# One fp32 transformer mixer layer on one core: another plan for sums of tokens, loads, the scale of q and the combining of output tiles

## The chip, the core and the metric

The kernel runs on one core of one Trainium2 chip. The metric is the time of one execution on the device in microseconds (us). The five engines are named as the profile names them: PE (TensorE, matrix products; PEld is its loading of weights), DVE (VectorE), ACT (ScalarE), POOL (GpSimd) and SP (SyncE, which here issues transfers only).

## What is computed

One layer over 512 tokens of 2048 channels, in fp32. Cut to what matters:

```python
h    = rms_norm(x, norm_g)
proj = h @ w_in                      # 512 x 2048 by 2048 x 8192
qa, ka, va, ga, qb, kb, vb, gb = split(proj)      # 8 + 8 heads of 128
ya = stick_breaking_attention(qa, ka, va)         # causal, no softmax
yb = chunk_band_attention(rms_norm(qb) , rms_norm(kb), vb, rel_bias)
mixed = concat(ya * silu(ga), yb * silu(gb))
out  = x + mixed @ w_out             # 512 x 2048 by 2048 x 2048
```

For the stick-breaking heads the weight of key s for query t is exp(log_sigmoid(z_ts) + the sum of log_sigmoid(-z_tj) over s < j < t). The chunked heads take a softmax over a band of nine chunks of 64 keys, with q and k normalised per head, gained, and a learned bias added.

## The kernel before

**Products.** Each fp32 operand is split into a high and a low part of type fp32r (`xh`, `xl` of the tokens, `wh`, `wl` of the weights), and a product is three matmuls, xh by wh, xl by wh and xh by wl (function `three`, lines 510 to 512). The two projections are made by a Winograd form of the 2x2 block product: seven products in the place of eight, of sums and differences of quarter blocks. The sums of weights (`wt`, lines 348, 351 and 352) and of tokens (`xt`, line 458, later split into `xh` and `xl` in lines 463 and 464) are made on DVE. ACT makes the high parts (line 370 for weights, 500 and 503 for tokens, where 503 multiplies by the norm's gain on the way), DVE the low parts (lines 374, 501 and 504).

**Units and steps.** The input projection has 32 units `u` of 256 output columns, four to a pair of heads (q, k, v, gate), the output projection four units of 512 columns (u = 32 to 35). A unit of the input projection has four steps (pairs j = 2r, 2r + 1 of the eight pairs of token tiles), one of the output projection eight. Units 0 and 1 are made in plain form and in turn, step by step, so that they need no sums of tokens (unit 32 is plain as well); unit 2 is the first that does. Weights of a step are loaded into one of three tiles `wt`, tokens of pair j into one of four staging tiles (`cq`, `ck`, `cv`, `cg`, which later hold the units' results). The four sums of pair j go into one tile, tag `v`, and the next pair's sums wait until they have been split.

**Results.** The products of a unit lie in halves of PSUM banks. Units 0, 1 and 32 are copied out by ACT (`copied`, line 625); all others are combined (`combine`): one ACT copy `U` (line 661), then six or seven DVE operations (lines 668, 676, 678, 679) that add and subtract the halves and free each for the unit that needs its bank next. The output projection has two row parts, a = 0 and 1, with tiles `wth` and `wtl` for results; x is added by transfers with accumulation that POOL issues (line 730), and SP stores the sum (line 735). For the last unit DVE and POOL add x.

**Attention.** While later units are multiplied, the heads of finished units are worked on: scores, for a stick-breaking head the chain ACT, POOL (a causal select, line 916), DVE scan (927), DVE subtraction (930), POOL select again, ACT exponential (933), then transposes on PE (1031), copies, and the product with the values. Sums of squares of x (`x_stats`, line 801) are made early on ACT from tiles `xs` that SP loads.

**Order.** There is no run-time scheduling. When the program is built, a planner simulates five engines and the transfers with a cost for each operation, and writes out a fixed order for each engine. An operation that is ready is taken by its due time; `need(k, d)` is the time at which product k will begin by the plan, less d, and `soon(d)` is d us from now. Costs on DVE and ACT are linear in the width. A transfer is planned to take its bytes by 330 bytes per ns, one after the other, and 2.2 us more to land. PE's next product is issued when its operands are there and nothing else is ready. An engine runs its list in order, and a wait of one instruction holds all that stand behind it.

The lines that matter most for what follows:

```python
WARM = 9                                                     # matmuls on zeros ahead of the first product
dma_free[0] = max(dma_free[0], clock[0] + op.cost) + op.lag / 330e3
return busy[engine] if op.quick else dma_free[0] + 2.2
yield lambda: "sums" not in done                             # sums of tokens: one tile
t = tmp([P, 4 * H], "v", f"xt{j}")
yield AC(H, lambda: act.activation(s_, s_, AF.Copy, scale=g_), need(k, 3.5))   # B12 of pair j
soon = lambda d: clock[0] + d                                # due time in combine
tag = ("wth", "wtl")[a]                                      # result tiles of the output projection
yield Op("SP", 0.94, gains, 25.0)                            # loads qg_t and kg_t
yield DV(1, lambda: dve.tensor_scalar(out=qgs, in0=qg_t, ...), 40.0)
```

Of the kernel before, what the change touches and what calls it, by code (L numbers as in the profile page):

```python
# [15 lines left out]
P = 128  # L16
# [43 lines left out]
WARM = 9  # L60
# [3 lines left out]
def trunk_kernel(ctx: ExitStack, tc: tile.TileContext, xT, xn, wi, wqk, wo, ng, qg, kg, rel, out):  # L64
# [62 lines left out]
    busy = dict.fromkeys(ready, 0.0)  # L127
    dma_free = [0.0]
# [44 lines left out]
    def issue(engine, op):  # L173
        op.fn()
        busy[engine] = clock[0] + op.cost
        if op.lag:
            dma_free[0] = max(dma_free[0], clock[0] + op.cost) + op.lag / 330e3

            return busy[engine] if op.quick else dma_free[0] + 2.2
        return busy[engine] + (0.17 if engine == "PE" else 0.1)  # L180

    def schedule(next_product):

        while True:
# [10 lines left out]
            for e in ready:  # L195
                if busy[e] > clock[0] + 1e-9:
                    continue
                if ready[e]:
# [140 lines left out]
    def landed_half(n, k, i, kk):  # L339
        at_ = dma_free[0] + 2.2  # L340
# [65 lines left out]
    def activations(j, mixed):  # L406
# [42 lines left out]
        else:  # L449
            yield lambda: "sums" not in done  # L450
            done.add("sums")
            t = tmp([P, 4 * H], "v", f"xt{j}")
# [3 lines left out]
            for o, i, g_, b_, op in ((0, 0, g1, q(r, 3), ALU.subtract), (1, 2, g2, q(r, 3), ALU.subtract),  # L456
                                     (2, 2, g2, q(t, 0), ALU.subtract), (3, 1, g2, q(t, 2), ALU.add)):
                yield DV(256, lambda: dve.scalar_tensor_tensor(out=q(t, o), in0=q(r, i), scalar=g_, in1=b_, op0=ALU.mult, op1=op,  # L458
# [7 lines left out]
        done.discard("sums")  # L466
# [27 lines left out]
    def raw_split(j, mixed, r, k, gain, x0, x1, names, h, l):  # L494
# [135 lines left out]
    def finish(u, a, t):  # L630
# [8 lines left out]
        done.remove(("co", a))  # L639

    def combine(u, a):
# [3 lines left out]
        soon = lambda d: clock[0] + d  # L645
# [17 lines left out]
        yield AC(512, first, soon(1))  # L663
# [4 lines left out]
        yield DV(256, lambda: dve.tensor_tensor(out=c[0][:, 1], in0=v(one(4)), in1=w[0], op=ALU.add), soon(1))  # L668
# [6 lines left out]
        else:  # L675
            yield DV(256, lambda: dve.tensor_tensor(out=c[0][:, 0], in0=w[0], in1=w[1], op=ALU.add), soon(1))
# [531 lines left out]
```

## Time and profile before

| what | value |
|---|---|
| median of three runs | 949.5 us (948.71 to 950.14) |
| the profiled execution | 950.14 us |
| its span, first to last instruction | 948.4 us |
| PE busy | 932.5 us (98%), 7377 matmuls |
| DVE busy | 830.0 us (88%) |
| ACT busy | 575.9 us (61%) |
| POOL busy | 80.3 us (8%) |
| granted TensorE clock, mean over the span | 0.997 |
| moved by transfers | 112.41 MB, 119 GB/s |

A busy share is an average over the whole span. The span is shorter than the execution's time by what lies before the first and behind the last instruction. PE counts as busy while any matmul is in flight, so that a PE that is busy all the time may still run at half of its clock; the granted clock of a stretch tells that.

### The profile page before, as it was taken

The numbers are of one execution on the slowest core, as the hardware profiler recorded it, in microseconds if no ns is written. First come the engines' busy times: TensorE is split into PE (matmuls) and PEld (weight loads), VectorE is DVE, ScalarE is ACT, GpSimd is POOL, SyncE is SP. The second block draws the span as 40 slices with busy tenths as digits, with TensorE's granted clock in tenths as the row PEclk, the third lists the DMA queues.
The fourth block names the chain that finished last, engine by engine and source line by source line (L and its number), as shares of the span: only waits on it lengthen the run. The fifth ranks groups of instructions, "written<-read, shape, count | busy, mean of one in ns | idle before, by whom it ended". The sixth has DMA issues, their size and how long they took to land.

```text
span 948.4 us, 19235 instructions
## 1 busy us (share of the span) xinstructions
PE 932.5 (98%) x7377; PEld 909.4 (96%) x7377; DVE 830.0 (88%) x1528; ACT 575.9 (61%) x1087; POOL 80.3 (8%) x157
## 2 busy tenths in 40 slices
PE   9899989999999999999999999999999999999997
PEld 7689989999999999999999999999999999999997
DVE  7789999988999989889999898899989987877875
ACT  6775856765467658654675576447768665534332
POOL 0001230000023000000230000002300000101010
PEclk9999999999999999999999999999999999999999
DMA  7742333223322332233223332422323445556471
GB/s 266 239 161 76 97 119 101 79 86 116 105 85 79 125 110 81 87 113 111 89 85 120 98 101 68 131 93 91 100 90 101 134 134 195 144 198 165 140 184 45
DMA packets 63916, 112.41 MB, mean 119 GB/s; under 512 B 7248, under 2 KB 11856, under 8 KB 63824
## 3 DMA queue, kind: packets, MB, share of 16 engines
q1 hardware_dynamic: 61680, 107.51, 35.2%
q0 software_dynamic: 1728, 3.15, 2.0%
q8 instruction: 57, 0.93, 0.4%
q10 hardware_dynamic: 416, 0.52, 0.2%
q14 instruction: 35, 0.29, 0.1%
HBM read 102.77 MB, written 8.39 MB: 117 GB/s over the span
## 4 chain that ended last, share of the span: by engine, by line
PE 56%; issue 27%; DVE 10%; DMA 4%; ACT 2%; POOL 1%; POOLq 0%; SPq 0%; DVEq 0%; ACTq 0%
PE banks L510 18%; PE banks L511 18%; PE banks L512 18%; DVE wl L374 3%; PE banks L1031 1%; DMA xs<-in_xn 1%; PE banks L959 1%; DMA co<-in_xn 1%; POOL W L916 1%; DMA x<-in_xT 1%; DVE wt L348 1%; ACT xs L801 1%; DMA qg_t<-in_qg 1%; DVE U L678 1%; DVE xt L458 0%
## 5 line engine op out<-in xcount | busy, mean ns | idle before, releaser
L510 PE MATMUL banks<-xh,wh 128*128 128x256 f32 (+1 forms) x1744 | 509.5, 292 | 3.2 <-ACT xh L500 1.6
L512 PE MATMUL banks<-xh,wl 128*128 128x256 f32 (+1 forms) x1744 | 501.3, 287 | 1.2 <-DVE wl L374 1.2
L511 PE MATMUL banks<-xl,wh 128*128 128x256 f32 (+1 forms) x1744 | 501.0, 287 | 0.5 <-DVE xl L501 0.5
L370 ACT CAST wh<-wt 128x1024 fp32r<-128x1024 f32 (+3 forms) x308 | 285.7, 937 | 242.4 <-PE banks L511 141.0
L374 DVE TENSOR_TENSOR wl<-wt,wh 128x768 fp32r<-128x768 f32 (+3 forms) x308 | 333.0, 1084 | 62.8 <-ACT wh L370 61.4
L510 PEld LDWEIGHTS banks<-xh,wh 128*128 128x128 f32 x1744 | 334.4, 192 | 7.8 <-ACT xh L500 2.4
L511 PEld LDWEIGHTS banks<-xl,wh 128*128 128x128 f32 x1744 | 334.2, 192 | 4.6 <-DVE xl L501 1.1
L512 PEld LDWEIGHTS banks<-xh,wl 128*128 128x128 f32 x1744 | 333.8, 191 | 5.0 <-DVE wl L374 2.4
L510 PE MATMUL banks<-wh,xh 128*128 128x256 f32 x432 | 122.7, 284 | 0.6 <-DVE co L679 0.5
L511 PE MATMUL banks<-wl,xh 128*128 128x256 f32 x432 | 122.3, 283 | 0.0
L512 PE MATMUL banks<-wh,xl 128*128 128x256 f32 x432 | 122.2, 283 | 0.0
L348 DVE TENSOR_TENSOR wt<-wt 128x512 f32<-128x512 f32 x144 | 99.4, 690 | 13.0 <-DMA wt<-in_wo 12.9
L510 PEld LDWEIGHTS banks<-wh,xh 128*128 128x128 f32 x432 | 82.9, 192 | 1.3 <-DVE co L679 1.2
L512 PEld LDWEIGHTS banks<-wh,xl 128*128 128x128 f32 x432 | 82.9, 192 | 0.0
L511 PEld LDWEIGHTS banks<-wl,xh 128*128 128x128 f32 x432 | 82.9, 192 | 0.0
L351 DVE TENSOR_TENSOR wt<-wt 128x256 f32<-128x256 f32 x144 | 61.1, 424 | 2.3
L352 DVE TENSOR_TENSOR wt<-wt 128x256 f32<-128x256 f32 x144 | 61.0, 424 | 2.0
L916 POOL TENSOR_SCALAR_AFFINE_SELECT W<-W 128x128 f32<-128x128 f32 x64 | 40.2, 629 | 98.4 <-DVE W L930 90.2
L916 POOL TENSOR_SCALAR_AFFINE_SELECT L<-L 128x128 f32<-128x128 f32 x32 | 21.8, 681 | 293.5 <-ACT L L922 286.3
L661 ACT COPY U<-banks 128x512 f32<-128x512 f32 x36 | 21.1, 585 | 23.9 <-PE banks L512 23.9
L1039 ACT CAST wth<-banks 128x128 fp32r<-128x128 f32 (+1 forms) x64 | 26.9, 421 | 10.4 <-PE banks L1031 10.4
L1031 PE MATMUL banks<-ident,W 128*128 128x128 f32 x160 | 29.2, 280 | 3.2 <-ACT W L933 2.5
(161 smaller groups left out, 1008.6 us busy)
## 6 DMA issues: line engine op xcount, KB each, us to landing
wt<-in_wi SPq DMA_DIRECT2D x254, 256.0 KB, 2.9
wt<-in_wo SPq DMA_DIRECT2D x64, 256.0 KB, 3.5
xs<-in_xn SPq DMA_DIRECT2D x16, 256.0 KB, 4.3
mixd<-c SPq DMA_DIRECT2D x16, 256.0 KB, 2.1
out<-co SPq DMA_DIRECT2D x16, 256.0 KB, 5.3
x<-in_xT SPq DMA_DIRECT2D x14, 256.0 KB, 4.5
co<-in_xn POOLq DMA_DIRECT2D x12, 256.0 KB, 7.2
bias<-in_rel SPq DMA_DIRECT2D x8, 256.0 KB, 3.3
```

Source lines behind the costliest of these rows:

```text
L348: yield DV(512, lambda: dve.tensor_tensor(out=some(t, 8, -7, 2), in0=some(t, 5, -5, 2), in1=some(t, 1, 0, 2), op=ALU.add), need(k0, 4))
L351: yield DV(256, lambda: dve.tensor_tensor(out=some(t, 9, 2), in0=some(t, 8, 2), in1=some(t, 0, 2), op=ALU.add), need(k1, 4))
L352: yield DV(256, lambda: dve.tensor_tensor(out=some(t, 12, 1), in0=some(t, 9, 2), in1=some(t, 4, 2), op=ALU.add), need(k1, 3.5))
L370: act.copy(whl[n, part][0][:, c], t)
L374: yield DV(c.stop - c.start, lambda: dve.tensor_tensor(out=l[:, c], in0=t, in1=h[:, c].bitcast(F32), op=ALU.subtract), need(k, 0.5))
L510: pe.matmul(o, lh, rh, start=start, stop=False, **kw)
L511: pe.matmul(o, lh, rl, start=False, stop=False, **kw)
L512: pe.matmul(o, ll, rh, start=False, stop=stop, **kw)
L661: act.copy(x[0], pair(u, a, 0, 1))
L916: pool.affine_select(out=x, in_=x, compare_op=ALU.is_gt, fill=fill, base=0, pattern=[[-1, P]], channel_multiplier=1)
L1031: pe.transpose(t[:, j * P:(j + 1) * P], src[:, j * P:(j + 1) * P], ident)
L1039: yield AC(w, lambda: act.copy(th[:, blocks, :], tv))
```

## The change

Eight edits, all in the planner's rules and costs or in where a value is kept; nothing else of the computation changes.

1. Eight matmuls on zeros ahead of the first product instead of nine.
2. Transfers are planned with 290 bytes per ns and 2.4 us to land. DVE operations with a scalar and two tensors (`STT`) are planned with 0.055 us more each.
3. The sums of tokens of pair j go into one of three tiles, `v`, `wth` or `wtl`, by j modulo 3. The first transposes of attention, which use `wth` and `wtl`, wait in turn for all eight pairs.
4. The scale of q's gain (`qgs`) is made only once 60 products have been issued.
5. The multiplication of the B12 part of pair 0 by the norm's gain goes from ACT to DVE.
6. In `combine` an operation that frees a bank is due by the next use of that bank (`next_use`), if that comes sooner than before.
7. After an operation of `combine` of the output projection, DVE takes for 0.2 us nothing that is due later than 1.5 us from then (`hold`).
8. Results of the output projection have four tiles: `wth` and `wtl` for even units, `cv` and `cg` for odd ones.

```diff
-WARM = 9
+WARM = 8
...
+    RATE, LANDING = 290e3, 2.4
...
+    def STT(w, fn, due=None):
+        return Op("DVE", 0.13 + 1.04e-3 * w, fn, due)
...
-            dma_free[0] = max(dma_free[0], clock[0] + op.cost) + op.lag / 330e3
-
-            return busy[engine] if op.quick else dma_free[0] + 2.2
+            dma_free[0] = max(dma_free[0], clock[0] + op.cost) + op.lag / RATE
+
+            return busy[engine] if op.quick else dma_free[0] + LANDING
...
+                    if clock[0] < held[e] - 1e-9 and k[0].due() > clock[0] + 1.5:
+                        continue
...
+                    if op.hold:
+                        held[e] = busy[e] + 0.2
+                        later(held[e], lambda: None)
...
-            yield lambda: "sums" not in done
-            done.add("sums")
-            t = tmp([P, 4 * H], "v", f"xt{j}")
+            tag = ("v", "wth", "wtl")[j % 3]
+            yield lambda: ("sums", tag) not in done
+            done.add(("sums", tag))
+            shape = [P, 2, S] if tag == "v" else [P, 13, P]
+            t = tmp(shape, tag, f"xt{j}").rearrange("p a b -> p (a b)")[:, :4 * H]
...
-                    yield AC(H, lambda: act.activation(s_, s_, AF.Copy, scale=g_), need(k, 3.5))
+                    if j:
+                        yield AC(H, lambda: act.activation(s_, s_, AF.Copy, scale=g_), need(k, 3.5))
+                    else:
+                        yield DV(H, lambda: dve.tensor_scalar(out=s_, in0=s_, scalar1=g_, scalar2=None, op0=ALU.mult), need(k, 3.5))
...
+    next_use, in_bank = {}, {}
+    for k in reversed(range(len(program))):
+        n, x, a = program[k]
+        u = steps_[n][0]
+        b = place(u, a, x[2]) // 2
+        if in_bank.get(b, (None, 0))[0] not in (None, (u, a)):
+            next_use[u, a, b] = in_bank[b][1]
+        elif b in in_bank and (in_bank[b][2] is not None):
+            next_use[u, a, b] = in_bank[b][2]
+        in_bank[b] = (u, a), k, next_use.get((u, a, b))
...
-            tag = ("wth", "wtl")[a]
-            yield lambda: ("co", a) not in done
-            done.add(("co", a))
+            tag = (("wth", "wtl"), ("cv", "cg"))[u % 2][a]
+            yield lambda: ("co", tag) not in done and emptied("cg", NG - 1)
+            done.add(("co", tag))
...
-        soon = lambda d: clock[0] + d
+        def soon(d, half=None):
+
+            t = clock[0] + d
+            k = None if half is None else next_use.get((u, a, place(u, a, half) // 2))
+            if k is None:
+                return t
+            wanted = need(k, 1.0)
+            return lambda: min(t, wanted())
...
+        def urgent(op):
+            op.hold = u >= NU
+            return op
...
-        yield DV(256, lambda: sub_(c[0][:, 1], v(one(6)), w[1]), soon(0.5))
+        yield urgent(DV(256, lambda: sub_(c[0][:, 1], v(one(6)), w[1]), soon(0.5, 6)))
...
-        yield lambda: ("turn", n, b - 1) in done if b else n == 0 or ("values", n - 1) in done
+        yield lambda: ("turn", n, b - 1) in done if b else ("values", n - 1) in done if n else all(("staged", j, 0) in done for j in range(NJ))
...
         yield Op("SP", 0.94, gains, 25.0)
+        yield lambda: position[0] > 60
         yield DV(1, lambda: dve.tensor_scalar(out=qgs, in0=qg_t, scalar1=SCALE, scalar2=None, op0=ALU.mult), 40.0)
```

What the planner makes of it is seen in the order of the instructions. At three places it is shown here; between the two kernels the line numbers differ (458 is 473 in the changed kernel, 464 is 479, 504 is 523, 501 is 520, 374 is 387, 348, 351 and 352 are 361, 364 and 365, 930 is 973).

**Place 1: DVE, in the steps of units 0 and 1.** `xl2` is the low part of token pair 2, `xt3` the sums of pair 3, `wl0_6` the low part of step 6's weights. Before:

```order
L464 TENSOR_TENSOR xl2_123<-xt2_333,xh2_122 128x1024
L1145 TENSOR_SCALAR qgs_72<-qg_t_70 128x1
L458 SCALAR_TENSOR_TENSOR xt3_396<-x3_124,ng_t_69 128x256 x2
L458 SCALAR_TENSOR_TENSOR xt3_396<-x3_124,ng_t_69,xt3_396 128x256 x2
L504 SCALAR_TENSOR_TENSOR xl6_367<-x6_365,ng_t_69,xh6_366 128x256
L501 TENSOR_TENSOR xl6_367<-x6_365,xh6_366 128x256
L464 TENSOR_TENSOR xl3_126<-xt3_396,xh3_125 128x1024
L374 TENSOR_TENSOR wl0_6_430<-wt6_286,wh0_6_429 128x1024
```

In the changed kernel:

```order
L473 SCALAR_TENSOR_TENSOR xt3_297<-x3_123,ng_t_69,xt3_297 128x256
L520 TENSOR_TENSOR xl5_236<-x5_234,xh5_235 128x256
L473 SCALAR_TENSOR_TENSOR xt3_297<-x3_123,ng_t_69,xt3_297 128x256
L387 TENSOR_TENSOR wl0_4_327<-wt4_249,wh0_4_326 128x1024
L523 SCALAR_TENSOR_TENSOR xl4_201<-x4_199,ng_t_69,xh4_200 128x512
L523 SCALAR_TENSOR_TENSOR xl5_236<-x5_234,ng_t_69,xh5_235 128x512
L473 SCALAR_TENSOR_TENSOR xt4_303<-x4_199,ng_t_69 128x256 x2
L473 SCALAR_TENSOR_TENSOR xt4_303<-x4_199,ng_t_69,xt4_303 128x256 x2
L479 TENSOR_TENSOR xl2_122<-xt2_222,xh2_121 128x1024
L479 TENSOR_TENSOR xl3_125<-xt3_297,xh3_124 128x1024
L387 TENSOR_TENSOR wl0_5_394<-wt5_275,wh0_5_393 128x1024
```

The last sum of pair 3 now stands ahead of step 4's weights and 14 rows ahead of the weights of step 6 (before 4 rows ahead of these); `qgs` stands 67 rows further down, behind the weights of step 12. SP's list at the same place, in the order of issue (`x7` is the load of pair 7, `wt8` of step 8). Before:

```order
L435 DMA x6_365<-in_xT 128x2x256
L436 DMA x6_365<-in_xT 128x512
L1141 DMA qg_t_70<-in_qg 128x1
L1142 DMA kg_t_71<-in_kg 128x1
L307 DMA wt8_382<-in_wi 128x512 x2
L796 DMA xs_393<-in_xn 128x512
L796 DMA xs_398<-in_xn 128x512
L796 DMA xs_409<-in_xn 128x512
L435 DMA x7_421<-in_xT 128x2x256
L436 DMA x7_421<-in_xT 128x512
```

In the changed kernel:

```order
L320 DMA wt6_313<-in_wi 128x512 x2
L448 DMA x6_317<-in_xT 128x2x256
L449 DMA x6_317<-in_xT 128x512
L448 DMA x7_344<-in_xT 128x2x256
L449 DMA x7_344<-in_xT 128x512
L320 DMA wt7_356<-in_wi 128x512 x2
L839 DMA xs_366<-in_xn 128x512
L839 DMA xs_369<-in_xn 128x512
```

Pair 7 is now loaded ahead of step 7's weights and of all tiles `xs`; before, step 8's weights and six tiles `xs` stood ahead of it.

**Place 2: DVE, where unit 34 ends and unit 35 begins.** `co34_1` is the result of unit 34's second row part, `wl0_153` and `wl1_153` belong to the second step of unit 35. Before:

```order
L679 TENSOR_TENSOR co34_1_11242<-banks_79,U_11233 128x2x128
L374 TENSOR_TENSOR wl0_153_11259<-wt153_11099,wh0_153_11258 128x1024
L678 TENSOR_TENSOR co34_1_11242<-banks_79,U_11233 128x2x128
L374 TENSOR_TENSOR wl1_153_11248<-wt153_11099,wh1_153_11247 128x768
L679 TENSOR_TENSOR co34_1_11242<-banks_79,U_11233 128x2x128
```

In the changed kernel:

```order
L721 TENSOR_TENSOR U_11230<-banks_79,co34_1_11239 128x512
L722 TENSOR_TENSOR co34_1_11239<-banks_79,U_11230 128x2x128
L721 TENSOR_TENSOR co34_1_11239<-banks_79,U_11230 128x2x128
L722 TENSOR_TENSOR co34_1_11239<-banks_79,U_11230 128x2x128
L387 TENSOR_TENSOR wl0_153_11257<-wt153_11096,wh0_153_11256 128x1024
L361 TENSOR_TENSOR wt154_11152<-wt154_11152 128x2x2x128
L387 TENSOR_TENSOR wl1_153_11245<-wt153_11096,wh1_153_11244 128x768
```

The two splits of weights have gone behind the last two operations that free banks.

**Place 3: DVE, behind the subtraction of the first stick-breaking head's third block of queries** (`W`, 384 keys), which POOL's second select waits for. Before:

```order
L930 TENSOR_TENSOR W_1099<-banks_79,W_1099 128x384
L348 TENSOR_TENSOR wt18_1080<-wt18_1080 128x2x2x128
L374 TENSOR_TENSOR wl1_17_1176<-wt17_1020,wh1_17_1175 128x768
L1117 TENSOR_TENSOR c3_1137<-c3_1137,R_78 128x1024
L883 TENSOR_TENSOR qk1_1205<-c0_537,qk1_1205 128x512
```

In the changed kernel:

```order
L973 TENSOR_TENSOR W_1129<-banks_79,W_1129 128x384
L365 TENSOR_TENSOR wt18_1059<-wt18_1059 128x256
L387 TENSOR_TENSOR wl0_18_1203<-wt18_1059,wh0_18_1202 128x1024
L361 TENSOR_TENSOR wt19_1110<-wt19_1110 128x2x2x128
L361 TENSOR_TENSOR wt20_1198<-wt20_1198 128x2x2x128
L364 TENSOR_TENSOR wt19_1110<-wt19_1110 128x2x128
L364 TENSOR_TENSOR wt20_1198<-wt20_1198 128x2x128
L365 TENSOR_TENSOR wt19_1110<-wt19_1110 128x256
```

Other operations follow the subtraction, and the transposes of this block stand 48 rows later in PE's list (row 648 instead of 600 of some 7120).

## Rows read from the trace of the kernel before

**Rows 1.** Busy time by stretch: PE, PEld, DVE, ACT, POOL, then granted clock, DMA, GB/s
```profile
30.00:40.00 10.00, 9.93 (x45) 7.91 (x43) 5.84 (x10) 6.24 (x13) 0.00 (x0) 1.00 0.86 257
40.00:50.00 10.00, 7.16 (x21) 4.98 (x22) 9.49 (x18) 7.71 (x19) 0.00 (x0) 0.83 0.73 245
50.00:60.00 10.00, 8.51 (x47) 7.21 (x45) 8.15 (x13) 7.69 (x16) 0.00 (x0) 1.00 0.57 181
60.00:100.00 40.00, 39.48 (x321) 38.75 (x322) 38.53 (x72) 24.00 (x42) 5.25 (x8) 1.00 0.30 99
100.00:150.00 50.00, 47.48 (x384) 46.42 (x383) 48.22 (x81) 35.91 (x68) 13.13 (x22) 1.00 0.30 96
150.00:200.00 50.00, 49.99 (x404) 48.93 (x403) 44.91 (x111) 35.05 (x95) 0.84 (x5) 1.00 0.31 96
```

**Rows 2.** Waits of PE: for whom, us in total, times, longest us
```profile
PE banks L1031 <- ACT W L933: 2.5, 2, 2.2
PE banks L510 <- ACT xh L500: 1.6, 1, 1.6
PE banks L510 <- ACT c L625: 1.5, 1, 1.5
PE banks L512 <- DVE wl L374: 1.2, 3, 0.7
PE banks L511 <- DVE xl L501: 0.5, 1, 0.5
```

**Rows 3.** Timeline of PE near 43 us: start, duration, instruction, idle before and releaser
```profile
43.47 0.49 PE L510 MATMUL banks<-xh,wh 128*128 128x512 f32 x1 [1.61 <-ACT xh L500]
```

**Rows 4.** Timeline of DVE near 36 us
```profile
35.96 0.15 DVE L1145 TENSOR_SCALAR qgs<-qg_t 128x1 f32<-128x1 f32 x1 [3.74 <-DMA qg_t<-in_qg]
```

**Rows 5.** Timeline of SP near 38 us
```profile
37.85 0.38 SPq L435 DMA_DIRECT2D x<-in_xT  x1
```

**Rows 6.** Timeline of ACT near 42 us and near 59 us
```profile
42.23 0.49 ACT L488 ACTIVATE x<-x,ng_t 128x256 f32<-128x256 f32 x1
...
58.81 0.63 ACT L801 ACTIVATE xs<-xs 128x512 f32<-128x512 f32 x1 [1.58 <-DMA xs<-in_xn]
...
59.43 0.57 ACT L625 COPY c<-banks 128x512 f32<-128x512 f32 x1
```

**Rows 7.** DMA issues by line (the page's part 6): KB each, median us to landing
```profile
xs<-in_xn SPq DMA_DIRECT2D x16, 256.0 KB, 4.3
```

**Rows 8.** Timeline of PE near 906 us
```profile
905.93 0.28 PE L512 MATMUL banks<-wh,xl 128*128 128x256 f32 x1
906.44 0.39 PE L510 MATMUL banks<-wh,xh 128*128 128x256 f32 x1 [0.23 <-DVE co L679]
```

**Rows 9.** Timeline of DVE near 905 us
```profile
905.10 0.94 DVE L374 TENSOR_TENSOR wl<-wt,wh 128x768 fp32r<-128x768 f32 x1
905.97 0.41 DVE L679 TENSOR_TENSOR co<-banks,U 128x256 f32<-128x256 f32 x1
```

**Rows 10.** Timeline of PE near 1 us and near 12 us
```profile
1.52 4.21 PE L1131 MATMUL banks<-zz 128*128 128x512 f32 x9 [1.52 <-DVE zz L1129]
...
12.79 0.50 PE L512 MATMUL banks<-xh,wl 128*128 128x512 f32 x1 [0.19 <-DVE wl L374]
```

**Rows 11.** Timeline of POOL near 120 us and near 140 us
```profile
120.68 2.42 POOL L916 TENSOR_SCALAR_AFFINE_SELECT W<-W 128x128 f32<-128x128 f32 x1 [4.16 <-DVE W L930]
...
140.21 1.15 POOL L916 TENSOR_SCALAR_AFFINE_SELECT W<-W 128x128 f32<-128x128 f32 x1 [2.06 <-DVE W L930]
```

**Rows 12.** Timeline of DVE near 122 us
```profile
120.47 0.41 DVE L351 TENSOR_TENSOR wt<-wt 128x256 f32<-128x256 f32 x1
120.80 1.22 DVE L374 TENSOR_TENSOR wl<-wt,wh 128x1024 fp32r<-128x1024 f32 x1
...
122.27 0.68 DVE L348 TENSOR_TENSOR wt<-wt 128x512 f32<-128x512 f32 x1
123.63 0.42 DVE L927 TENSOR_TENSOR_SCAN W<-L,W 128x128 f32<-128x128 f32 x1 [0.68 <-POOL W L916]
```

More of the change, by code (lines that the diff above doesn't have):

```diff
@@ L127, in trunk_kernel @@
     busy = dict.fromkeys(ready, 0.0)
+    held = dict.fromkeys(ready, 0.0)
     dma_free = [0.0]
@@ L139, in __init__ @@
             self.due = due if callable(due) else (lambda d=clock[0] + LATE if due is None else due: d)
+            self.hold = False
     LATE = 5.0
+    RATE, LANDING = 290e3, 2.4
     def DV(w, fn, due=None, n=1):
@@ L457, in activations @@
                                      (2, 2, g2, q(t, 0), ALU.subtract), (3, 1, g2, q(t, 2), ALU.add)):
[L458 removed]
+                yield STT(256, lambda: dve.scalar_tensor_tensor(out=q(t, o), in0=q(r, i), scalar=g_, in1=b_, op0=ALU.mult, op1=op,
                                                               reverse1=op == ALU.subtract), need(kt, dt + 4))
@@ L465, in activations @@
         done.update(("x", j, x, mixed) for x in ("T1", "T2", "T3", "T4"))
-        done.discard("sums")
+        if not mixed:
+            done.remove(("sums", tag))
         names = ("B11", "B21") + (("B12",) if not mixed or plain(NU, j) else ())
@@ L503, in raw_split @@
             yield AC((x1 - x0) * H, lambda: act.activation(h, s_, AF.Copy, scale=gain), need(k, 2.6))
-            yield DV((x1 - x0) * H, lambda: dve.scalar_tensor_tensor(out=l, in0=s_, scalar=gain, in1=h.bitcast(F32), op0=ALU.mult,
+            yield STT((x1 - x0) * H, lambda: dve.scalar_tensor_tensor(out=l, in0=s_, scalar=gain, in1=h.bitcast(F32), op0=ALU.mult,
                                                                     op1=ALU.subtract), need(k, 0.5))
@@ L661, in first @@
             act.copy(x[0], pair(u, a, 0, 1))
-        yield AC(512, first, soon(1))
+        yield AC(512, first, soon(1, 0))
         w = [v(x[0][:, i, :]) for i in range(2)]
@@ L667, in combine @@
         c, t = yield from result(u, a)
-        yield DV(256, lambda: dve.tensor_tensor(out=c[0][:, 1], in0=v(one(4)), in1=w[0], op=ALU.add), soon(1))
+        yield urgent(DV(256, lambda: dve.tensor_tensor(out=c[0][:, 1], in0=v(one(4)), in1=w[0], op=ALU.add), soon(1, 4)))
         free(4)
@@ L675, in combine @@
         else:
-            yield DV(256, lambda: dve.tensor_tensor(out=c[0][:, 0], in0=w[0], in1=w[1], op=ALU.add), soon(1))
+            yield urgent(DV(256, lambda: dve.tensor_tensor(out=c[0][:, 0], in0=w[0], in1=w[1], op=ALU.add), soon(1)))
         yield there(2, 3)
@@ L679, in combine @@
         add_ = lambda o, i, j: dve.tensor_tensor(out=o, in0=i, in1=j, op=ALU.add)
-        yield DV(512, lambda: sub_(v(x[0]), v(pair(u, a, 2, 3)), c[0][:, 1][:, None].to_broadcast(list(v(x[0]).shape))), soon(1))
+        yield urgent(DV(512, lambda: sub_(v(x[0]), v(pair(u, a, 2, 3)), c[0][:, 1][:, None].to_broadcast(list(v(x[0]).shape))), soon(1, 2)))
         free(2)
-        yield DV(256, lambda: add_(c[1][:, 1], v(one(3)), w[0]), soon(1))
+        yield urgent(DV(256, lambda: add_(c[1][:, 1], v(one(3)), w[0]), soon(1, 3)))
         free(3)
@@ L685, in combine @@
             yield there(5)
-            yield DV(256, lambda: add_(c[1][:, 1], c[1][:, 1], v(one(5))), soon(1))
+            yield urgent(DV(256, lambda: add_(c[1][:, 1], c[1][:, 1], v(one(5))), soon(1)))
             free(5)
@@ L709, in combine @@
         yield there(7)
-        yield DV(256, lambda: add_(c[1][:, 0], v(one(7)), w[0]), soon(0.2))
+        yield urgent(DV(256, lambda: add_(c[1][:, 0], v(one(7)), w[0]), soon(0.2, 7)))
         free(7)
@@ L877, in prep_a @@
         if kind == 0:
-            yield DV(512, lambda: dve.scalar_tensor_tensor(out=f, in0=f, scalar=SCALE, in1=R, op0=ALU.mult, op1=ALU.mult))
+            yield STT(512, lambda: dve.scalar_tensor_tensor(out=f, in0=f, scalar=SCALE, in1=R, op0=ALU.mult, op1=ALU.mult))
         else:
@@ L989, in prep_b @@
         yield AC(512, lambda: act.activation(d[:, 2 * kind, :], b, AF.Copy, scale=gain))
-        yield DV(512, lambda: dve.scalar_tensor_tensor(out=d[:, 2 * kind + 1, :], in0=b, scalar=gain, in1=d[:, 2 * kind, :].bitcast(F32),
+        yield STT(512, lambda: dve.scalar_tensor_tensor(out=d[:, 2 * kind + 1, :], in0=b, scalar=gain, in1=d[:, 2 * kind, :].bitcast(F32),
                                                       op0=ALU.mult, op1=ALU.subtract))
```

8 lines of the change are left out of this document (4 added, 4 removed).

## The prediction

> **What bounds the kernel now.** I read the page first: PE is busy 98% of the span, so time can only be won where PE stands or runs slowly. The stretches come next [rows 1]. From 30 to 40 us PE issues 45 matmuls of 512 columns in 10 us, one each 0.222 us, and from 150 to 200 us 404, nearly all of 256 columns, one each 0.124 us. Two stretches fall out: 40 to 50 us, with 21 matmuls, 7.16 us busy and a mean granted clock of 0.83 of 2.4 GHz, which is part of the stretch at 1.2 GHz; and 50 to 60 us, with 1.49 us idle. From 100 to 150 us 2.5 us are idle. The waits of PE say for whom [rows 2]: a low part of weights (three times, 1.2 us in all), token pair 7 (1.6 and 0.5 us), a copy of unit 1's result (1.5 us), an exponential of attention (two, 2.5 us).
>
> The reader is to follow the stop at 43.47 us back. PE waits for the high part of pair 7 [rows 3]; ACT began on pair 7 at 42.23 us [rows 6], since SP issued that load only at 37.85 us [rows 5], into the staging tile that pair 3 had to leave. Pair 3 is left when DVE has made its sums, and DVE came to them at 36 us: it had stood 3.74 us for a transfer of 512 bytes, q's gain, of which it makes `qgs`, a value first used in a chunked head much later [rows 4]. While PE stood its clock fell, and the matmuls after the stop ran at half of it.
>
> **The change, part by part.**
>
> *A. The early stop (edits 2, 3, 4).* `qgs` goes down 67 rows; nothing early then waits on that transfer. Sums in three tiles let pair 3's sums go ahead of step 4's weights, and SP issues pair 7 ahead of step 7's weights. The queues it moves past: on SP, the weights of steps 7 and 8 and six tiles `xs` now come after it; weights have three tiles and are loaded two steps ahead of their use, which hides that. On DVE the sums move ahead of weights that are needed later. Price of the stop: 45 less 21 matmuls are missing, 24 x 0.222 = 5.3 us [rows 1]. Bounds: 0 if another input is late in its place, 5.3 if none. I take 5.3: all three causes are moved by more than a step (24 matmuls of 0.222, 5.3 us), and DVE gets its 3.74 us back.
>
> *B. The copy of unit 1 (edit 2).* ACT stood 1.58 us for a tile `xs` and made the copy only at 59.43 us, for which PE waited 1.5 us [rows 2, 6]. The transfer takes 4.3 us [rows 7] and was planned with some 3.0 (262144 bytes by 330 per ns, and 2.2); 290 and 2.4 give 3.3, nearer but still short. Of the 16 squares 13 stood ahead of that copy, the last of them directly; now nine do, with a cast of weights between. Bounds 0 and 1.6 (1.5, and the longer matmul behind a stop); I take 1.2, nearer the upper end, since four transfers less must land before it.
>
> *C. Ends of units 33 and 34 (edits 6, 7, 8).* PE issues a matmul at 905.93 us and the next at 906.44, 0.51 instead of 0.124 later, and waits for DVE's last addition at 905.97 [rows 8]. Ahead of that stood a split of weights of 0.94 us [rows 9], and a longer one further ahead; both now stand behind it. 0.39 us a boundary, and 0.11 because the first matmul after a stop is longer (0.39 against 0.28): two boundaries, 1.0 us. Bounds 0 and 1.0; I take 1.0, since the addition comes 0.94 us or more sooner for a wait of 0.39. The two splits, of the next step's weights, are late next. Three sums of a later step's weights have gone from ahead of the first split (0.68, 0.42 and 0.41 us by their like in [rows 12]), more than the two additions that came ahead of it. The second split is needed eight products of three matmuls into its step, 24 x 0.124 = 3 us; without that cover PE would wait up to 0.94 us. Four result tiles hide nothing, as no row shows a wait for a result tile; edit 8 is 0.
>
> *D. The start (edits 1, 5).* Nine matmuls on zeros take 4.21 us, 0.47 each [rows 10]. But PE waits at 12.79 us for a low part of step 1's weights, ahead of which DVE has 18 operations before and 20 after, with one moved from ACT [rows 10]. DVE begins sooner by the ACT operation that has gone (0.49 for its like in [rows 6]) and has about as much more to do. So 0; bounds -0.5 (slower) and +0.5.
>
> *E. Attention's first heads (follows from all).* PE stood 2.2 us for an exponential, because POOL's select took 2.42 us, and another took 1.15 us [rows 2, 11]. While the first was held, DVE ran four operations with both operands in SBUF, the first at 120.47 and the last at 122.27 us, and then stood 0.68 us itself for that select [rows 12]. The new order deals these anew: other operations follow each subtraction. Bounds: +2.5 if no select is held, -8.1 if all three long runs hold one (the rival below). I take +1.0: of the eight subtractions of the first two heads two cost something before, 2.2 and 0.3 us, and I put in one stop between them, 1.5.
>
> The Trainium skill (page "SBUF — State Buffer", section "SBUF: two separate sides") says that a DVE instruction with two SBUF inputs and a GpSimd instruction that reads SBUF lock each other out, and that the later one waits for the whole instruction of the other. The trace agrees that POOL is blocked, but its 2.42 us go past the end of one DVE instruction of 1.22 us and into a fourth. By the rule a hold would end after 1.22 us at most, an estimate of 0.6 on the mean; PE's wait would be some 0.4 us instead of 1.5, and the forecast 1.1 us lower.
>
> *F. New short waits.* The first 60 us are dealt anew. The nearest row are the three waits for weights, 1.2 us in all [rows 2]; bounds 0 and 3.6, three times as many. I take one more such set, -1.2.
>
> Sum: 5.3 + 1.2 + 1.0 + 0 + 1.0 - 1.2 = 7.3 us off the profiled execution, whose span is 948.4 and whose time is 950.14 us. The median of the three runs is 949.5, 0.6 lower; taken from it, **942.2 us**. The end is untouched: the last PE matmul to the last store keep their order.
>
> **Rivals.**
>
> *DVE takes it back.* PE gets 5.3 + 1.2 - 1.2 = 5.3 us sooner into a stage where DVE is nearly full: idle 1.5 us of 40 and 1.8 of 50 [rows 1]. If DVE has only these 3.3 us to give until 150 us, 2.0 come back as waits for weights, and E's 1.0 is lost: 949.5 - 7.3 + 3.0 = 945.2. For it: 96% busy. Against: DVE also has the 3.74 us it stood, 5.1 us idle from 150 to 200, and the planner put attention later against the products (48 rows of PE, 6 us, at place 3), and level with before by about 200 us.
>
> *Another late input takes the place of pair 7.* Then A is lost and the rest stays: 949.5 - 7.3 + 5.3 = 947.5. For it: transfers still land later than planned, by 1.0 us for `xs`, and the transfer engines are 0.86 busy from 30 to 40 us [rows 1]. Against: pairs 5, 6 and 7 are each issued a step or more ahead.
>
> *The change gains nothing.* The edits move a plan, not work. If the rest of the program waits on loads, an earlier PE meets later weights, and only C stays: 948.5. For it: transfers land later than the plan has it, 4.3 against 3.3 us for `xs` [rows 7]. Against: the transfer engines are 0.31 busy from 150 to 200 us [rows 1], and no row of PE's waits names a transfer.
>
> *Slower: held selects.* In the new order three subtractions of the first two stick-breaking heads are followed by at least four operations with both operands in SBUF (by the durations of [rows 12], with 0.94 for a split of 768 columns [rows 9], 3.7, at least 4.2 and 3.3 us). If POOL is held through each, PE waits each time for 0.2 us less, as it did (2.2 of 2.42): 10.6 us instead of 2.5, E is -8.1 instead of +1.0, and DVE's own stops of 0.68 us make its weights late by 2.0 more: 949.5 - 7.3 + 9.1 + 2.0 = 953.3. It decides from 9.2 us of such waits on beyond the 1.5 in E. Against: such a run stood behind the third subtraction before as well (place 3), and only two waits are on record [rows 2].
>
> **How the numbers follow.** Forecast 0.65, DVE takes it back 0.13, another late input 0.08, nothing gained 0.07, slower 0.07. 0.2% are 1.9 us, about what a measurement of this kernel can tell from no change. Faster by more, below 947.6: the first two and three quarters of the third, 0.84. Within: the rest of the third and the fourth, 0.09. Slower: 0.07. The low end has A, the upper bounds of B, C and E and no new waits: 949.5 - 5.3 - 1.6 - 1.0 - 2.5 = 939.1, and with D's bound 938.6. The high end takes in the third case, 947.5. What lies outside is the fourth and fifth case and some of the third. The forecast's own range is 938.6 to 945.
>
> **What would show it.** A: from 40 to 50 us no clock below 1.00, some 45 matmuls of 512 columns, no wait for pair 7, `qgs` without a wait. B: no wait of PE for the copy of unit 1. C: PE's pitch at the two ends of units stays 0.12 us, DVE's splits behind the additions. D: PE's first products up to 0.5 us sooner, the wait near 12.8 us still there. E: selects above 1 us, and waits of PE for an exponential between 80 and 150 us. Wrong it would be with a second clock drop in the first 70 us, waits for low parts of weights between 60 and 200 us of over 2 us in all, or several selects above 2 us with PE behind them.

## The result, and the profile after

The changed kernel takes 942.65 us (median of 4, 942.48 to 942.99) against 949.71 us before on the same chip (4 runs, 948.71 to 950.14): ratio 0.9928, 95% interval 0.991 to 0.9945. Forecast were 942.2 us in 938.6 to 947.5. The profiled execution takes 942.50 us, its span is 940.4 us.

The page's header and busy line of the changed kernel:

```profile
span 940.4 us, 19231 instructions
PE 929.5 (99%) x7376; PEld 908.0 (97%) x7376; DVE 830.7 (88%) x1529; ACT 574.1 (61%) x1085; POOL 79.4 (8%) x157
```

Busy shares hardly move. The stretches, with the columns of [rows 1], changed kernel:

```profile
30.00:40.00 10.00, 10.00 (x45) 8.26 (x45) 9.38 (x17) 6.53 (x16) 0.00 (x0) 1.00 0.67 195
40.00:50.00 10.00, 10.00 (x46) 8.27 (x45) 10.00 (x16) 9.90 (x20) 0.00 (x0) 1.00 0.66 219
50.00:60.00 10.00, 10.00 (x82) 9.88 (x81) 9.93 (x16) 8.73 (x15) 0.00 (x0) 1.00 0.74 239
60.00:100.00 40.00, 39.56 (x327) 39.11 (x326) 38.25 (x74) 24.48 (x46) 5.36 (x11) 1.00 0.34 116
100.00:150.00 50.00, 49.22 (x397) 48.05 (x396) 46.00 (x80) 33.99 (x67) 14.73 (x19) 1.00 0.29 97
150.00:200.00 50.00, 49.31 (x392) 47.75 (x392) 43.50 (x110) 34.96 (x96) 0.84 (x5) 1.00 0.27 86
```

From 40 to 50 us there are 46 matmuls and a clock of 1.00, where [rows 1] have 21 and 0.83. From 50 to 60 us PE is never idle. But from 150 to 200 us it issues 392 instead of 404. PE's waits, columns as in [rows 2], changed kernel:

```profile
PE banks L1074 <- ACT W L976: 1.8, 6, 0.4
PE banks L529 <- DVE wtl L1083: 0.5, 1, 0.5
PE banks L531 <- DVE wl L387: 0.2, 1, 0.2
```

The waits for pair 7 and for the copy of unit 1, both in [rows 2], are gone. Two waits for an exponential, one of them 2.2 us long, have become six of at most 0.4 us.

To add this up I use PE's **lost time**: for each matmul the time from its start to the next one's start, less the median of that for its shape in the same trace, summed by stretch. It counts idle time, the longer first matmuls behind a stop, and matmuls at half clock alike. Worked out from the trace of every kernel here (us; the heads of the columns are us from the span's start, the last column is the span):

```
kernel              0-20  20-50  50-66 66-150 150-300 300-800  800-   all    span
before              3.46   5.60   1.78   4.52   1.56   4.24   1.57  22.73   948.4
changed             3.79  -0.04  -0.01   2.52   3.73   4.61   0.29  14.88   940.4
only_tiles          3.75  -0.05  -0.01   2.81   1.79   4.27   1.38  13.95   939.7
only_q_later        3.40   1.85   1.99   4.90   1.54   4.26   1.38  19.32   945.0
only_combine        3.57   4.15   3.55   6.00   1.54   4.25   0.06  23.12   948.8
q_from_ng           3.60   2.28   3.60   5.96   1.56   4.29   1.38  22.67   948.4
xs_later            3.81   0.94   0.31   9.68   2.93   4.29   1.35  23.31   949.0
q_ng_xs_later       3.63  -0.04   0.04   8.93   2.89   4.28   1.35  21.08   946.8
tiles_combine       3.58  -0.04  -0.01   5.01   1.74   4.14   0.06  14.48   940.2
undo_tiles          3.20   2.51  -0.01   1.96   1.70   4.37   0.59  14.32   939.8
undo_combine        3.90  -0.04  -0.01   3.20   3.74   4.52   2.79  18.09   943.6
undo_plan           3.59  -0.04  -0.01   3.46   1.75   4.35   0.06  13.16   938.6
undo_plan_select    3.61  -0.04   0.55   1.96   1.01   3.81   0.05  10.95   936.4
```

Lost time falls by 7.85 us, the span by 8.0: the table accounts for the gain. Each row is one execution, and not always a middling one: that of `only_q_later` took 946.73 us with a granted clock of 0.999, its median is 950.07.

### The profile page after: what moved, and what is told of

Its sections match the earlier page's. It is cut to its first block, busy times and chain, and to the rows that moved or that the text cites. A ratio compares the mean times of both kernels' runs of the same rounds, so it can differ in the third digit from the quotient of the medians.

```text
span 940.4 us, 19231 instructions
## 1 busy us (share of the span) xinstructions
PE 929.5 (99%) x7376; PEld 908.0 (97%) x7376; DVE 830.7 (88%) x1529; ACT 574.1 (61%) x1085; POOL 79.4 (8%) x157
## 4 chain that ended last, share of the span: by engine, by line
PE 61%; issue 24%; DVE 10%; ACT 2%; POOL 2%; DMA 0%; ACTq 0%; DVEq 0%; POOLq 0%
PE banks L529 19%; PE banks L530 19%; PE banks L531 19%; DVE wl L387 3%; POOL W L959 1%; PE banks L1074 1%; PE banks L1002 1%; DVE wt L361 1%; DVE W L970 1%; ACT wh L383 1%; DVE wtl L1083 1%; DVE wt L364 1%; PE banks L1110 0%; DVE W L973 0%; DVE wt L365 0%
## 5 line engine op out<-in xcount | busy, mean ns | idle before, releaser
L387 DVE TENSOR_TENSOR wl<-wt,wh 128x1024 fp32r<-128x1024 f32 (+3 forms) x308 | 333.9, 1085 | 69.7 <-ACT wh L383 65.7
L1083 DVE TENSOR_TENSOR wtl<-banks,wth 128x128 fp32r<-128x128 f32 (+1 forms) x64 | 30.8, 482 | 2.0 <-ACT wth L1082 2.0
```

The source lines that it names most:

```text
L387: yield DV(c.stop - c.start, lambda: dve.tensor_tensor(out=l[:, c], in0=t, in1=h[:, c].bitcast(F32), op=ALU.subtract), need(k, 0.5))
L1083: yield DV(w, lambda: dve.tensor_tensor(out=tl[:, blocks, :], in0=tv, in1=th[:, blocks, :].bitcast(F32), op=ALU.subtract))
```

## The experiments

The experiments were timed in three sets, on chips 12, 2 and 1, each with the kernel before beside it: 951.29, 951.26 and 950.89 us (medians of 26, 8 and 19 runs). Ratios are to that, with 95% intervals. The first set has `only_tiles`, `only_q_later`, `only_combine` and `q_from_ng`, the second `tiles_combine`, `undo_tiles`, `undo_combine` and `undo_plan`, the third the other four.

### Which edit takes the early stop away

**One edit alone, on the kernel before.** `only_tiles` is edit 3:

```diff
-            yield lambda: "sums" not in done
+            tag = ("v", "wth", "wtl")[j % 3]
+            yield lambda: ("sums", tag) not in done
```

> The kernel before with edit 3 alone, sums in three tiles. DVE still stands for q's gain. Theory: the sums of pair 3 are made before that stand, so pair 7 is loaded in time, but the low parts behind the stand are late: 1 to 3 us gained. Rival (the tiles are the cause): 4 to 5 us gained and no clock drop.

Measured: 942.04 us (941.37 to 944.16), ratio 0.9917 [0.9888, 0.9946]. `only_q_later` is edit 4:

```diff
+        yield lambda: position[0] > 60
         yield DV(1, lambda: dve.tensor_scalar(out=qgs, in0=qg_t, ...), 40.0)
```

> The kernel before with edit 4 alone, the scale of q made only once 60 products have been issued. Theory: like the run without the wait, 3 to 5 us gained. Rival (three tiles are needed): less than 2 us gained, pair 7 still the last to come.

Measured: 950.07 us (946.73 to 952.68), ratio 0.9994 [0.9974, 1.0014]. `only_combine` is edits 6, 7 and 8:

> The kernel before with edits 6, 7 and 8 alone (due by the bank's next use, hold, four result tiles). Theory: PE's stops at the ends of units 33 and 34 go, 1.0 to 1.5 us gained, the early stop stays. Rival: nothing gained, since the order around the first heads changes as well and gives it back.

Measured: 949.83 us (946.63 to 951.63), ratio 0.9991 [0.9972, 1.001]. The tiles alone give the whole early gain, more than the 4 to 5 us of the rival: lost time from 20 to 66 us is nil. By the ratio they give as much as all eight edits (0.9913 for the changed kernel in these sets, below). The other two can't be told from no change; the gain of 3 to 5 us that was expected of edit 4 did not come. SP's timeline of `only_tiles` (the load of pair 7 is two rows, lines 435 and 436):

```profile
25.30 0.38 SPq L435 DMA_DIRECT2D x<-in_xT  x1
25.72 0.47 SPq L436 DMA_DIRECT2D x<-in_xT  x1
...
27.61 1.38 SPq L799 DMA_DIRECT2D xs<-in_xn  x3
```

Pair 7 is issued 12.5 us sooner than in [rows 5], ahead of all tiles `xs`. Edit 4 alone still leaves a stop there, of 1.25 us.

**The stand for q's gain, by itself.** `q_from_ng` keeps before's order, and reads another operand, so that DVE doesn't wait (the scale of q in the chunked heads is another number):

```diff
-        yield DV(1, lambda: dve.tensor_scalar(out=qgs, in0=qg_t, scalar1=SCALE, ...), 40.0)
+        yield DV(1, lambda: dve.tensor_scalar(out=qgs, in0=ng_t[:, 0:1], scalar1=SCALE, ...), 40.0)
```

> The kernel before, with the same order on every engine; only the value qgs is made from a column of ng_t, which landed long before, in the place of q's gain (so the scale of q in the chunked heads is another number). Theory: DVE's stand of 3.74 us for that transfer is what made pair 7 late; without it the clock drop at 44 us goes and 3 to 5 us with it (945 to 947 us). Rival 1 (sums in one tile hold pair 3): the stop stays over half, less than 2 us gained. Rival 2 (the transfer of pair 7 is late by itself): nothing gained.

Measured: 949.16 us (946.71 to 952.25), ratio 0.9983 [0.9962, 1.0003]. SP, ACT and PE of `q_from_ng` (start, duration, instruction, idle before and releaser):

```profile
33.02 1.63 SPq L796 DMA_DIRECT2D xs<-in_xn  x3
35.06 0.38 SPq L435 DMA_DIRECT2D x<-in_xT  x1
...
38.79 0.63 ACT L801 ACTIVATE xs<-xs 128x512 f32<-128x512 f32 x1 [0.78 <-DMA xs<-in_xn]
...
39.73 0.63 ACT L801 ACTIVATE xs<-xs 128x512 f32<-128x512 f32 x1 [0.21 <-DMA xs<-in_xn]
...
40.41 0.63 ACT L801 ACTIVATE xs<-xs 128x512 f32<-128x512 f32 x1
...
41.11 0.51 ACT L488 ACTIVATE x<-x,ng_t 128x256 f32<-128x256 f32 x1
...
42.36 0.49 PE L510 MATMUL banks<-xh,wh 128*128 128x512 f32 x1 [1.69 <-ACT xh L500]
```

The load is issued 2.8 us sooner than in [rows 5], and PE still stands 1.69 us; the theory's 3 to 5 us did not come. Three loads of `xs` go out just ahead of pair 7, and on ACT the three squares (line 801) of these tiles stand ahead of pair 7's first operation (line 488), two of them waiting for their own transfers. The kernel before has the same three squares there, which I had not read:

```profile
40.39 0.61 ACT L801 ACTIVATE xs<-xs 128x512 f32<-128x512 f32 x1
...
41.00 0.61 ACT L801 ACTIVATE xs<-xs 128x512 f32<-128x512 f32 x1
...
41.62 0.61 ACT L801 ACTIVATE xs<-xs 128x512 f32<-128x512 f32 x1
```

Pair 7's operation follows at 42.23 us [rows 6]. By then its load had landed:

```profile
x<-in_xT SPq DMA_DIRECT2D x2, 256.0 KB, 3.1
```

Issued at 37.85 us, it was there near 41 us. So of PE's 1.61 us some 1.3 are the squares' (an estimate from these rows), and in the kernel before the load's own time adds little.

**Queue and stand crossed.** `xs_later` lets the squares start later, `q_ng_xs_later` does that and `q_from_ng`'s edit (so q's scale is another number there too):

```diff
-        yield lambda: position[0] > 18
+        yield lambda: position[0] > 33
```

> The kernel before, with the loads of the sixteen tiles xs allowed only from product 33 on instead of 18: on SP no tile xs stands ahead of the load of pair 7; q's scale still waits for its transfer, and sums of tokens still have one tile. Queue (the transfers ahead of pair 7 in the queue make it late): the load lands 3 us after its issue or sooner, and the early stop near 40 us falls below 0.5 us with no clock drop; about 946. Stand (DVE's wait for q's gain makes it late): it is issued near 37.8 us all the same, and the stop stays at 1 us or more, with the drop behind it; 949 to 951. Staging (pair 7 can be issued only when pair 3's sums are made, whatever the queue holds): issued at 35 to 38 us, landed about 3 us later, the stop between 0.5 and 1.5 us.

Measured: 950.57 us (949.21 to 951.28), ratio 0.9994 [0.9978, 1.0011].

> The same, with the scale of q made from the norm's gain, which is there from the start (the scale of q in the chunked heads is another number), so that DVE doesn't stand at 36 us. Queue and stand together: pair 7 is issued near 35 us and lands near 38, no early stop above 0.3 us, no clock drop before 60 us: 944 to 946. If one tile for sums of tokens alone makes pair 7 late, a stop above 1 us stays near 40 us and the time is 948 or more.

Measured: 948.66 us (948.50 to 949.88), ratio 0.9979 [0.9965, 0.9993]. First `xs_later`, SP, ACT and PE:

```profile
36.38 0.38 SPq L435 DMA_DIRECT2D x<-in_xT  x1
...
39.08 0.51 ACT L488 ACTIVATE x<-x,ng_t 128x256 f32<-128x256 f32 x1 [1.63 <-DMA x<-in_xT]
...
41.80 0.50 PE L511 MATMUL banks<-xl,wh 128*128 128x512 f32 x1 [0.69 <-DVE xl L501]
```

Then the same of `q_ng_xs_later`, where no matmul from 20 to 60 us waits, and further down the place that takes the gain back:

```profile
34.86 0.38 SPq L435 DMA_DIRECT2D x<-in_xT  x1
...
37.73 0.51 ACT L488 ACTIVATE x<-x,ng_t 128x256 f32<-128x256 f32 x1 [1.33 <-DMA x<-in_xT]
...
119.33 0.50 PE L510 MATMUL banks<-qk 128*128 128x512 f32 x1 [1.71 <-DVE wtl L1040]
...
122.95 0.90 PE L1031 MATMUL banks<-ident,W 128*128 128x128 f32 x3 [2.65 <-ACT W L933]
```

The two loads of pair 7 take 6.1 us to land in `q_from_ng` and 2.9 us here, by the DMA view of the stretch in which each is issued (`q_from_ng`, then `q_ng_xs_later`):

```profile
x<-in_xT SPq DMA_DIRECT2D x2, 256.0 KB, 6.1
```

```profile
x<-in_xT SPq DMA_DIRECT2D x2, 256.0 KB, 2.9
```

In `q_from_ng` the gain of 2.8 us in issue went into the queue (it lands near 41 us, as in the kernel before) and ACT's squares. The four lost times from 20 to 50 us are 5.60 with both causes, 2.28 without the stand, 0.94 without the squares and their loads, -0.04 without either. The 5.60 hold some 1.6 us of matmuls at half clock (one each 0.43 us instead of 0.22), which in `q_from_ng` come only behind its next stop; from 20 to 66 us, with that stop (for unit 1's copy), the four are 7.38, 5.88, 1.25 and 0.00. So there are two causes, and the squares with their loads are the larger. They are not independent: with the loads out of the way q's gain landed sooner too, and DVE's stand in `xs_later` is only 1.30 us:

```profile
33.88 0.15 DVE L1145 TENSOR_SCALAR qgs<-qg_t 128x1 f32<-128x1 f32 x1 [1.30 <-DMA qg_t<-in_qg]
```

How much of the delay is the squares' on ACT and how much their loads' on SP was not tried. Both theories were half right. The third reading, staging, has the issue (36.38 us) and the stop (0.69 us) of `xs_later` right, but `q_ng_xs_later`, with one tile as before, has no stop: one tile is not enough to make pair 7 late. Yet neither kernel is much faster: from 66 to 150 us they lose 9.7 and 8.9 us instead of 4.5. In the order that the later squares leave, two blocks' transposes stand with one product of three matmuls between them, so that PE waits 1.71 and 2.65 us for the chain of attention, and from 120 to 130 us the granted clock falls to 0.66:

```profile
120.00:130.00 10.00, 7.02 (x39) 6.16 (x38) 9.10 (x17) 5.95 (x10) 1.53 (x3) 0.66 0.13 40
```

This is the slower rival's place (a stop before the transposes), through another door: the planner's order there, not a held second select (POOL's took 0.62 us). Whether a first select held for 3.31 us at 101.65 us had a part in it is not shown.

### What each group of edits is worth in the changed kernel

**Edits 3 and 6 to 8 alone** (`tiles_combine`, on the kernel before):

> The kernel before with edits 3, 6, 7 and 8 (three tiles for sums, rules of combining), without the new transfer times, the later scale of q and the start. Theory (tiles carry the early stop and the copy, combining the two ends of units, the other edits nothing or less): the ratio of edit 3 alone and 1.5 us less, span about 938.3 us. Rival (the other edits are needed to keep the order tight): 940.4 us or more, as with all edits.

Measured: 941.47 us (940.79 to 942.01), ratio 0.9897 [0.9873, 0.992]. Two groups are enough; the other four edits add nothing that can be measured. But the theory's span, 938.3 us, was not reached (940.2), and the combining edits add too little to edit 3 alone (0.9917) to be told from nothing.

**Without the three tiles** (`undo_tiles`, edit 3 of the changed kernel undone):

> All edits but the three tiles for sums; the rule that attention's first transposes wait for all pairs stays. Theory: pair 7 is loaded late again, a stop of 1.5 to 3 us near 42 us comes back and the copy of unit 1 waits, 5 us or more slower than with all edits (span 945 or more). Rival (longer transfer times in the plan and the later scale of q are enough): within 1.5 us of all edits.

Measured: 942.25 us (941.51 to 943.28), ratio 0.9906 [0.9882, 0.993]. The 5 us did not come; the rival, within 1.5 us of all edits, did. SP, ACT and PE of `undo_tiles`:

```profile
21.31 0.38 SPq L448 DMA_DIRECT2D x<-in_xT  x1
...
29.29 0.51 ACT L502 ACTIVATE x<-x,ng_t 128x256 f32<-128x256 f32 x1
...
30.55 0.49 PE L526 MATMUL banks<-xh,wh 128*128 128x512 f32 x1 [1.38 <-ACT xh L516]
31.43 0.50 PE L527 MATMUL banks<-xl,wh 128*128 128x512 f32 x1 [0.39 <-DVE xl L517]
...
35.17 0.38 SPq L448 DMA_DIRECT2D x<-in_xT  x1
```

The stop has moved to pair 5: PE stands 1.38 and 0.39 us for it, 2.51 lost, and no clock drop follows. Now PE is later, and pair 7, issued at 35.17 us, is in time. The some 2.5 us that it loses there come back in part from 150 to 300 us (1.70 against 3.73). My expectation priced the stop with its clock drop, and left out that attention is dealt anew.

**Without the combining edits** (`undo_combine`, edits 6, 7 and 8 undone):

> All edits but 6, 7 and 8. Theory: stops of 0.4 and 0.5 us come back at each end of units 33 and 34, span 1.0 to 1.5 us longer than with all edits (941.4 to 941.9). Rival: same or shorter, since the due times by the bank's next use also moved attention and gave that back.

Measured: 945.08 us (944.92 to 946.08), ratio 0.9942 [0.9916, 0.9968]. PE's waits and one of the two stops, and DVE's order ahead of it:

```profile
PE banks L529 <- DVE co L722: 2.0, 2, 1.0
...
860.00 0.38 PE L529 MATMUL banks<-wh,xh 128*128 128x256 f32 x1 [1.00 <-DVE co L722]
...
856.26 1.21 DVE L387 TENSOR_TENSOR wl<-wt,wh 128x1024 fp32r<-128x1024 f32 x1
857.40 0.41 DVE L722 TENSOR_TENSOR co<-banks,U 128x256 f32<-128x256 f32 x1
857.73 0.94 DVE L387 TENSOR_TENSOR wl<-wt,wh 128x768 fp32r<-128x768 f32 x1
```

Two splits stand between the additions, as in [rows 9], but here each boundary costs 1.16 us instead of 0.39.

**Without the other rates and costs** (`undo_plan`, edit 2 undone):

```diff
-    RATE, LANDING = 290e3, 2.4
+    RATE, LANDING = 330e3, 2.2
...
-        return Op("DVE", 0.13 + 1.04e-3 * w, fn, due)
+        return Op("DVE", 0.075 + 1.04e-3 * w, fn, due)
```

> All edits but the planned times of transfers and of DVE operations with a scalar (330 bytes per ns, 2.2 us, no 0.055 us). Theory (they move little that PE waits for): span within 1 us of all edits (939.4 to 941.4), no wait of PE for a copy of unit 1. Rival (the prediction's term B): PE waits 0.5 to 1.5 us for that copy again, 941.5 to 942.5.

Measured: 940.77 us (939.84 to 941.52), ratio 0.9889 [0.9865, 0.9913]. No wait for the copy of unit 1 comes back, and lost time from 150 to 300 us is 1.75 instead of 3.73. The span, 938.6 us, is below both ranges. The changed kernel itself, in the third set:

> The changed kernel as it is, in the same set of runs as the three beside it. If edit 2 costs time, it is 1.0 to 2.0 us slower than without edit 2 (942 to 943, ratio to before 0.989 to 0.992); if the kernel without edit 2 only had a better chip, it is 940.5 to 941.5.

Measured: 942.22 us (942.11 to 944.20), ratio 0.9913 [0.988, 0.9947]. The runs of the two do not overlap, their ratios' intervals do, and they are of two sets: edit 2 costs about 1.5 us by the medians, 1.8 by the spans, which is likely but not settled.

**A dearer select** (`undo_plan_select`: edit 2 undone, and POOL's second select planned dearer):

```diff
-            yield G(0.35, lambda: causal(W[:, d], NEG_BIG))
+            yield G(0.9, lambda: causal(W[:, d], NEG_BIG))
```

> The changed kernel with before's rates for transfers and costs on DVE (edit 2 undone, the fastest so far at 940.8), and POOL's second select planned at 0.9 us instead of 0.35. If the stops behind held selects can be planned away, those from 80 to 140 us and near 260 us lose 1 to 2 us together: 939 to 940. If a dearer select only deals the order anew, stops of the same sum stand elsewhere: 940.5 to 942.5.

Measured: **937.0 us** (936.01 to 938.13), ratio 0.9854 [0.9821, 0.9887], the fastest kernel here: its slowest run is below the fastest of `undo_plan` and of the changed kernel, and its median is below both ranges. The select that was planned dearer takes at most 1.22 us with either price; one of 3.14 us is a first select, whose price is the same. But PE waits less for the exponential behind it (`undo_plan`, then `undo_plan_select`):

```profile
PE banks L1074 <- ACT W L976: 1.1, 2, 0.8
```

```profile
PE banks L1074 <- ACT W L976: 0.2, 1, 0.2
```

Two stretches of `undo_plan_select`:

```profile
100.00:150.00 50.00, 49.82 (x405) 48.94 (x404) 48.74 (x87) 35.16 (x69) 9.01 (x20) 1.00 0.30 101
200.00:300.00 100.00, 99.94 (x822) 99.15 (x821) 92.18 (x151) 61.24 (x96) 12.03 (x25) 1.00 0.29 96
```

From 66 to 300 us lost time is 2.97 us, against 5.21 in `undo_plan`; the span falls as much (2.2 us). Some 0.9 us of that are the waits above. The rest may be the price's or luck of the new order: in the kernels here lost time in that stretch goes from 2.97 to 12.61 us, and `undo_tiles`, without the dearer price, has 3.66.

## Why the prediction was right, and where its reasons were not

The sum was 7.3 us off the profiled execution; 7.64 came off it (950.14 to 942.50), 7.06 off the medians.

- **A, 5.3 us: right in size (5.64), incomplete in its cause.** The step "DVE came to them at 36 us: it had stood 3.74 us for ... q's gain" names one of two causes, and "ACT began on pair 7 at 42.23 us, since SP issued that load only at 37.85 us" misses that ACT was at the squares when the load landed. With the stand gone 2.28 us are still lost; ACT's three squares ahead of pair 7, and their loads ahead of it on SP, are the other cause and the larger. Edit 3 alone removes both, since it brings pair 7 ahead of them; edit 4 adds nothing to it. Nor is edit 3 needed beside the others: `undo_tiles` gains as much by the time.
- **B, 1.2 us: 1.79, more than the upper bound of 1.6; attribution wrong.** It was put down to edit 2; `undo_plan` has the gain without it, and `only_tiles` has it with edit 3 alone: there ACT makes three squares before 51.2 us, and the next only behind both copies of the unit.
- **C, 1.0 us: 1.28 in the changed kernel, 1.5 by `only_combine`.** The mechanism holds, DVE's splits now stand behind the additions. The time of `only_combine` doesn't show the gain: from 20 to 150 us 1.8 us more are lost than before. In the plan with the other edits the same group is worth 2.9 us by the time (945.08 less 942.22, of two sets), more than the 1.0 to 1.5 that were expected of undoing it. What each of the three edits does was not tried.
- **D, 0: -0.33, inside its bounds.** The wait near 12.8 us is still there, at 12.91.
- **E, +1.0, and F, -1.2: together -0.2, measured -0.54.** But they lie elsewhere. From 66 to 150 us 2.0 us are won; the short waits of F, put into the first 60 us, did not come there (`wl`: 0.2 us in all); 2.2 us are lost from 150 to 300 us, which no step named. That their sum is near is luck, and so is part of the whole: B, C and A came out higher, D, E and F lower.

**The slower rival** was right on POOL for one of its three runs, and wrong on PE. In the changed kernel, POOL's select, three of DVE's operations in that time, the exponential on ACT, and PE:

```profile
101.29 6.11 POOL L959 TENSOR_SCALAR_AFFINE_SELECT W<-W 128x128 f32<-128x128 f32 x1 [3.45 <-DVE W L973]
...
101.42 1.21 DVE L387 TENSOR_TENSOR wl<-wt,wh 128x1024 fp32r<-128x1024 f32 x1
...
105.10 0.95 DVE L387 TENSOR_TENSOR wl<-wt,wh 128x768 fp32r<-128x768 f32 x1
105.97 1.28 DVE L926 TENSOR_TENSOR qk<-c,qk 128x512 fp32r<-128x512 f32 x2
...
107.43 0.53 ACT L976 ACTIVATE W<-W 128x384 f32<-128x384 f32 x1 [1.97 <-POOL W L959]
...
108.01 0.55 PE L1074 MATMUL banks<-ident,W 128*128 128x128 f32 x3 [0.19 <-ACT W L976]
```

The select is held for 6.11 us, through eleven DVE operations with both operands in SBUF, one behind the other (the last ends at 107.25), longer than the 4.2 us that the rival could count for it. PE waits 0.19 us for it, since its transposes now stand 48 rows further down (place 3): the two moves cancel. No other second select is held over 1.5 us. The Trainium skill (page "SBUF — State Buffer", section "SBUF: two separate sides") says that the instruction that starts first gets the shared ports for the whole of that instruction. By that rule the hold would end with one DVE instruction, and this row does not agree: the longest of them is 1.21 us, and the select ended only behind the whole run.

**DVE takes it back** did not decide: with edit 3 alone, PE is as far ahead and loses less from 66 to 150 us than before (2.81 against 4.52).

## What to carry to other kernels

Follow a late operand back on every queue it passes, not only to the first stand that is long enough to explain it: here the load's place in the queue, ACT's own list and DVE's stand each held it, and removing the stand or the squares alone moved the time by nothing that could be measured, while sending the load out ahead of all three gave the whole gain. A change of plan deals all later stages anew, so a clean gain of 5 us early can vanish 80 us later; compare kernels by lost time per stretch before putting a price on an edit. Where an operation is held by something that the planner does not know, a dearer price for it in the plan is worth a try: that one constant went with 2.2 us by the spans and 3.8 by the medians (of two sets), in one case, and how much of it is the price's own is open.

## What was not expected of the hardware

**The clock and the spread.** A stop of PE of about 2 us is followed by a lower clock in some places and not in others. In the kernel before the granted clock is 0.83 from 40 to 50 us, where PE stood 1.61 us just behind another wait of 0.71, but 1.00 behind stops of 1.54 us (to 60.05) and 2.22 us (to 123.82). In `q_from_ng` it is 1.00 behind one of 1.69 us (to 42.36), but 0.89 from 50 to 66 us, with one of 1.87 us (to 57.21). Its stop of 2.22 us near 122 us, at the same matmul as in the kernel before, is followed by a lower clock that the other does not have (the kernel before, then `q_from_ng`, columns as in [rows 1]):

```profile
120.00:130.00 10.00, 7.78 (x62) 7.45 (x61) 8.67 (x17) 5.49 (x11) 4.00 (x5) 1.00 0.44 133
```

```profile
120.00:130.00 10.00, 7.78 (x49) 7.44 (x49) 7.19 (x15) 5.40 (x11) 3.20 (x5) 0.83 0.37 126
```

Of 53 runs of the kernel before in the three sets, the 10 with a mean granted clock of 0.998 or 0.999 took 946.5 to 949.5 us, the 16 with 0.993 took 951.8 to 953.7. The changed kernel has 0.998 to 1.000 in all eight runs. So part of its gain in those sets, an estimate of some 3 us (the kernel before's medians of 950.9 to 951.3 less 947.9, the median of those ten), is clock that it no longer loses, and its runs lie closer together. Why the same stop lowers the clock in one run and not in the next stays open.

**Landing.** The same load of pair 7 took 2.9 us to land in `q_ng_xs_later`, with no `xs` queued ahead of it, and 6.1 us in `q_from_ng`, with three of them issued in the some 2 us before it. Here no one time to land fits.
